# Six plain up tiles kept in SBUF, and the adaLN halves of the w_o stage spread over earlier stages

## The chip, the cores and the metric

One core of one Trainium2 chip. The metric is the device time of one execution in microseconds; the kernel before was run three times, and its median counts. Beside the times stands a profile of one execution, with every instruction's engine, source line, start and duration. Its engines are PE (TensorE, matrix products), PEld (its weight loads), DVE (VectorE), ACT (ScalarE), POOL (GpSimd, here an issuer of DMAs) and SP (SyncE, which issues most DMAs). An engine works its instructions off in the order in which they were compiled; an instruction that waits holds all behind it on its engine.

## What is computed

One layer of a decoder trunk for 512 tokens and 2048 channels, in float32: a mixing sub-layer (two attention groups) and a gated MLP with a short causal convolution, each with adaLN modulation from a vector `c`.

```python
mod = silu(c) @ w_ada + b_ada                   # six rows of 2048: sh1, sc1, gt1, sh2, sc2, gt2
h = rmsnorm(x, g_mix) * (1 + sc1) + sh1
x = x + (1 + gt1) * mixer(h, ...)               # ends in: merged @ w_o
h = rmsnorm(x, g_ffn) * (1 + sc2) + sh2
u = h @ w_up                                    # 2048 x 11264
u = conv_b + conv_w[0]*u[t-2] + conv_w[1]*u[t-1] + conv_w[2]*u[t]
a, b = split(u)
x = x + (1 + gt2) * ((silu(a) * b) @ w_down)
out = rmsnorm(x, g_final)
```

The last row of `mod` (gt2) is made in another place (`last_gate`) and is not touched.

## The kernel before

**Products.** Activations lie channels by tokens (128 x 512 tiles). Each float32 product is made of three passes on high and low parts (`mm3`, lines 176 to 180). A weight piece of 128 x 1024 comes by a DMA from SP into one of eight `raw` buffers; ACT copies its high part into `wh` (L168), and DVE subtracts to get `wl` (L170); there are three rooms of `wh` and `wl`, used in turn.

**A unit** (`unit`, lines 242 to 315) makes two output tiles `c1` and `c2` from two columns of weights and the 16 operand tiles, by seven half-size products of 24 matmuls with 256 columns each (a Strassen-like scheme). It loads four weight quarters `a11`, `a21`, `a22`, `a12` and keeps a fifth `raw` buffer `s` for sums of them (L268, L272; L306 and L310 work in place). It evacuates with ACT (L266, L270, L304) and DVE (L276, L308, L309, L312, L314). Twice, after its second product and after its fourth, it calls `between(i, *pins)`, where other stages hang side work; `behind(*pins)` places that work in its engine's order behind the named instructions. PSUM has three banks `acc`, four `att` and one `outs`; units use `acc` and `att` in turn.

**Order.** The program is traced in the order of the code, and a scheduler at compile time fixes each engine's order, by priority of tracing and by when operands and free buffers are expected. A tile gets a buffer of its tag when one is free: `raw` has eight, `F` (from `slot()`) 62 of 128 x 512, `T` two. The operand forms of a unit stage hold 56 of the 62 slots.

**adaLN halves.** `mod` is computed by DVE: a row tile of `w_ada` (128 x 1024, half of one of 48 tiles) is loaded into a `raw` buffer (`ada_load`, L702) and multiplied and summed against `cb[half]` (`some_ada`, L711). There are 96 halves from `ada_left`, first halves first. `cb[1]`, the second half of silu(c) on all partitions, takes one `raw` buffer from the first second half to the last. Before the change, 31 of them are done in the w_x units (one per unit), 7 through the `soft` buffer beside them, 15 in the stick-breaking heads 0 to 4, 26 in the sparse heads, 6 in the w_b stage and the last 11 in the w_o units (`between`, lines 1119 to 1123, up to two per unit).

**Stages, in order:** values and index queries (to about 232 us), 31 w_x units (to about 826), indexer and values (`indexer`, lines 873 to 880), eight stick-breaking heads (to about 1003), eight sparse heads with `branch_a` beside them (to about 1138), w_b, eight w_o units (first evacuation at 1235), the first up stage, 41 up units (first evacuations from 1478 to 2266), the down stages.

**First up stage** (lines 1223 to 1295). Six up tiles (three `a`, three `b` tiles, 2 x `NU`) are made by plain products in six PSUM banks (`ups`). ACT evacuates them to slots (L405), and POOL saves them to DRAM (`ud`, L1295). Later `finish_first` brings each back by SP's queue (L1337), applies the convolution (L1330 on ACT, L1333 twice on DVE), Silu (L1346), the product of the pair (L1352), and saves the result to `yd`. One step of it is traced per up unit from j = 9 on, 27 steps in all.

**Up units** (lines 1357 to 1364). For each pair the unit's outputs go through `finish` (convolution L1210 on ACT, L1211 and L1212 on DVE, Silu L1217, product L1219). `beside_up` hangs a step of `last_gate` and `turn` into each call; `turn` transposes an x1 tile (four transposes into `outs`) and frees its slot. Tiles 14 and 15 are read back from DRAM into `T` buffers for that at j = 6 and 7; tile 13 is still in a slot when the w_o stage ends and is turned in the first up unit.

Of the kernel before, what the change touches and what calls it, by code (L numbers as in the profile page):

```python
# [14 lines left out]
AF = mybir.ActivationFunctionType  # L15
ALU = mybir.AluOpType
# [4 lines left out]
S = 512  # L21
KT = D // P
# [14 lines left out]
NU = 3  # L37
# [39 lines left out]
def block_kernel(ctx: ExitStack, tc: tile.TileContext, A: dict, out: bass.AP):  # L77
    nc = tc.nc
# [10 lines left out]
    def t2k(tag, bufs, dt=F32, w=S):  # L89
        return sb.tile([P, w], dt, tag=tag, bufs=bufs, name=nm(tag))  # L90

    def slot(dt=F32):

        return t2k("F", SLOTS, dt)
# [11 lines left out]
    act = nc.scalar.activation  # L106
    tt = nc.vector.tensor_tensor
    ts = nc.vector.tensor_scalar
    stt = nc.vector.scalar_tensor_tensor
# [213 lines left out]
    @contextmanager  # L323
    def behind(*pins):

        with ExitStack() as stack:
            for p in pins:
                stack.enter_context(tc.issue_after(p.ins))
            yield
# [73 lines left out]
    def evac(ps, rows=slice(0, P), scale=None):  # L403
        o = slot()
        act(o[rows], ps[rows], AF.Copy, **({} if scale is None else {"scale": scale}))  # L405
        return o
# [6 lines left out]
    for k in range(KT):  # L413
# [4 lines left out]
        t = KT + k  # L418
# [4 lines left out]
        x = xt[k]  # L423
# [34 lines left out]
    dram = lambda name, n, w=S: [dr.tile([P, w], F32, tag=f"{name}{i}", name=f"{name}{i}") for i in range(n)]  # L458
    save = nc.gpsimd.dma_start
# [18 lines left out]
    for k in range(KT):  # L478
# [4 lines left out]
        if k == 0:  # L483
# [3 lines left out]
            w = w_next  # L487
        else:
            with behind(*([ada_tile(k + 1)] if k + 1 < KT else [])):
                tt(lo, xt[k], hi.bitcast(F32), ALU.subtract)  # L490
            w = prep(A["w_qi"][k])
# [20 lines left out]
    ps = acc()  # L512
    for c in range(2):
        w = prep(A["w_tail"][c], 8 * TN)
# [12 lines left out]
    for j, (src, dst) in enumerate(((A["w_x0"][0], xd[0]), (A["w_x0"][1], xd[1]))):  # L527
        ps = (acc, att)[j % 2]()
        for c in range(2):
            w = prep(src[c])  # L530
            for k in range(8):
                i = 8 * c + k
# [162 lines left out]
    def ada_load(n=1, tag=("raw", 8)):  # L695
        for _ in range(min(n, len(ada_left))):
            t, half = ada_left.pop(0)
            if half and cb[1] is None:
                cb[1] = t2k("raw", 8, w=1024)
                nc.sync.dma_start(cb[1], c_half.to_broadcast([P, 1024]))  # L700
            w = t2k(*tag, w=1024)
            nc.sync.dma_start(w, A["w_ada"][t * P : (t + 1) * P, half * 1024 : (half + 1) * 1024])  # L702
            ada_ready.append((w, t, half))

    def some_ada(n=1):
        for _ in range(n):
            if not ada_ready:
                ada_load()
            if ada_ready:
                w, t, half = ada_ready.pop(0)  # L710
                stt(w, w, 1.0, cb[half], ALU.mult, ALU.mult, accum_out=macc[:, t, half : half + 1])  # L711
# [36 lines left out]
    for u in range(1, 32):  # L748

        def between(i, *pins):  # L750
            if not i:
                ada_load()
            with behind(*pins):
                next(work)
                if i:
                    some_ada()

        pair = unit(A["w_x"][u - 1], f, between)
        for i, o in enumerate(pair):
            if u >= 16:  # L760
                sig = act(o, o, AF.Sigmoid)
            save(xd[2 * u + i], o)
# [42 lines left out]
    bias = [causal]  # L805
# [61 lines left out]
    def run(work, n=1):  # L867
        for _ in range(n):
            last = next(work, None)
        return last  # L870
# [4 lines left out]
    run(index)  # L875
    fill = values(0, vb[0])
    for i in range(16):
        run(fill, 2)
        run(index)
    run(fill)  # L880


# [136 lines left out]
    def sparse_3(p):  # L1019
        tps = [acc() for _ in range(3)]  # L1020
        tp = strips(*tps)
        pT = t2k("w", 2), t2k("T", 2), t2k("T", 2)
        for b in (2, 0, 1, 3):
            for kb in range(b + 1):
                nc.tensor.transpose(tp[b][:, kb * P : (kb + 1) * P], p[b][:, kb * P : (kb + 1) * P], ident)
        for n in (1, 2, 0):
            W = (S, S, 2 * P)[n]
            act(pT[n][:, :W], tps[n][:, :W], AF.Copy)
        return strips(*pT)
# [27 lines left out]
    for hd in range(NH):  # L1057
        ada_load(2 if hd > 1 else 0)
        p, s, last = sparse_1(*pairs[hd])
        if before:  # L1060
            sparse_4(*before, y)
        if hd + 1 < NH:
            pairs.append(turned(hd + 1))
        run(fill)
        with behind(last):
            some_ada(2 if hd > 1 else 0)
        ada_load(2 if hd else 0)
        last = sparse_2(p, s)
        run(fill)
        before = hd, sparse_3(p), vb[hd // 4]  # L1070
        with behind(last):
            some_ada(2 if hd else 0)
        run(fill, 2)
    sparse_4(*before, y)
    run(fill)
# [7 lines left out]
    for j in range(KT):  # L1083
        t = t2k("w", 2)
# [3 lines left out]
        ps = acc()  # L1088
        w = prep(A["w_b"][j])
# [16 lines left out]
    to_turn = []  # L1106

    def turn():

        if to_turn:  # L1110
            j, x = to_turn.pop(0)
            ps = outs()
            for b in range(NQB):
                nc.tensor.transpose(ps[:, b * P : (b + 1) * P], x[:, b * P : (b + 1) * P], ident)
            o = slot()
            act(o, ps, AF.Copy)
            save(x1t[:, :, j * P : (j + 1) * P], o.rearrange("p (b f) -> p b f", b=NQB))

    def between(i, *pins):
        turn()  # L1120
        with behind(*pins):
            some_ada()
        ada_load()

    def residual(c, j, x, at=slice(0, S)):
        stt(c[:, at], c[:, at], mod[:, 32 + j : 33 + j], x[:, at], ALU.mult, ALU.add)
# [163 lines left out]
    for form in (form_t, form_u):  # L1290
        for p in range(KT // 2 - LAG, KT // 2):
            form(f[p], x1[2 * p], x1[2 * p + 1])
    ud = dram("ud", 2 * NU)
    for i, ps in enumerate(ups):
        save(ud[i], evac(ps))  # L1295

    gate_row = dr.tile([1, D], F32, tag="gate", name="gate")
    gate_sum = [dr.tile([P, 1024], F32, tag=f"gates{half}", name=f"gates{half}") for half in range(2)]
# [1 line left out]
    def last_gate():  # L1300
# [9 lines left out]
        for b in range(4):  # L1310
# [7 lines left out]
            save(gate_row[:, b * S : (b + 1) * S], w[:1, S:])  # L1318
            yield

    def beside_up(i, *pins):
        turn()
        with behind(*pins):
            run(gate)

    def finish_first():

        def half(j, u):
            t = t2k("T", 2)
            act(t, u, AF.Identity, scale=cw[:, j, 2:3], bias=cw[:, j, 3:4])  # L1330
            for i in (1, 2):
                yield t
                stt(t[:, i:], u[:, : S - i], cw[:, j, 2 - i : 3 - i], t[:, i:], ALU.mult, ALU.add)  # L1333

        def bring(i):
            u = slot()
            nc.sync.dma_start(u, ud[i])  # L1337
            return u

        for j in range(NU):  # L1340
            u = bring(2 * j)
            yield
            yield
            for a in half(2 * j, u):
                yield
            act(a, a, AF.Silu)  # L1346
            u = bring(2 * j + 1)
            yield
            yield
            for b in half(2 * j + 1, u):  # L1350
                yield
            tt(a, a, b, ALU.mult)  # L1352
            save(yd[j // 2][:, j % 2 * S : (j % 2 + 1) * S], a)
            yield

    gate, first_tiles = last_gate(), finish_first()
    for j in range(NU, NJ):
        if 2 * NU <= j < 2 * NU + 2:
            x = t2k("T", 2)
            save(x, x1d[KT - 2 + j - 2 * NU])  # L1360
            to_turn.append((KT - 2 + j - 2 * NU, x))
        if j >= 3 * NU:
            run(first_tiles)
        finish(j, *unit(A["w_up"][j - NU], f, beside_up))


# [365 lines left out]
```

## Time and profile before

| what | value |
|---|---|
| median of three runs | 2738.51 us (2733.37 to 2740.41) |
| the profiled execution | 2737.63 us |
| its span, first to last instruction | 2735.7 us |
| granted TensorE clock, mean | 0.995 |
| TensorE matmuls | 18700 |
| issues of `w_ada` rows into `raw` | 152 of 512 KB |
| issues to and from `ud` | 6 and 6 of 256 KB |

How to read the rows below: a windows row gives a stretch of the span, its length, each engine's busy time with the number of instructions, the granted clock, the DMA engines' share and their rate. A row of the lines or the waits view names the line, engine and tiles; `X <- Y: 5.2, 2, 2.9` says that X waited for Y 5.2 us in total, two times, 2.9 us at most. A timeline row gives start, duration, engine, line, operation, and in brackets the engine's idle time before it and what ended that.

### The profile page before, as it was taken

How to read it: one execution, taken by the hardware profiler on the slowest of the kernel's cores; microseconds unless marked ns; L12 is line 12 of the kernel's file. 1: busy time of each engine (PE TensorE's matmuls, PEld its weight loads, DVE VectorE, ACT ScalarE, POOL GpSimd, SP SyncE). 2: the span in 40 equal slices, each digit the busy share in tenths (PEclk: the TensorE clock that was granted, in tenths of full speed). 3: DMA queues.
4: the chain of work that ended last, by engine and by line, in shares of the span. 5: the costliest groups of instructions: out<-in, count | busy, mean ns of one | idle time of the engine just before them, and what ended most of it. 6: DMA issues, size and time to landing. Idle time of an engine off the chain costs nothing.

```text
span 2735.7 us, 47661 instructions
## 1 busy us (share of the span) xinstructions
PE 2677.8 (98%) x18700; PEld 2453.8 (90%) x18700; DVE 2406.6 (88%) x3402; ACT 1448.4 (53%) x2037; POOL 315.8 (12%) x514
## 2 busy tenths in 40 slices
PE   8999999999999999999999999999999999999998
PEld 6789999999997778889999999999999998887876
DVE  8888989999987899798878999999999997888887
ACT  4444455554446665434466555555555455546443
POOL 0000010100012211112220000000000000003011
PEclk9999999999999999999999999999999999999999
DMA  9883556666676648766864666666666436468785
GB/s 351 326 301 123 174 199 196 192 212 220 205 227 203 199 140 285 237 206 216 243 215 136 189 175 189 173 181 175 171 177 181 132 125 223 154 179 236 207 228 166
DMA packets 167853, 551.65 MB, mean 202 GB/s; under 512 B 21750, under 2 KB 22390, under 8 KB 167628
## 3 DMA queue, kind: packets, MB, share of 16 engines
q1 hardware_dynamic: 119820, 408.49, 46.4%
q0 software_dynamic: 47216, 139.73, 18.7%
q8 instruction: 147, 2.41, 0.3%
q14 instruction: 78, 0.64, 0.1%
q10 hardware_dynamic: 592, 0.39, 0.1%
HBM read 453.97 MB, written 91.14 MB: 199 GB/s over the span
## 4 chain that ended last, share of the span: by engine, by line
PE 83%; DVE 8%; DMA 4%; issue 3%; ACT 2%; SPq 0%; POOL 0%; ACTq 0%; DVEq 0%; POOLq 0%
PE att L180 13%; PE att L179 13%; PE att L178 13%; PE acc L179 12%; PE acc L180 12%; PE acc L178 12%; DVE wl L170 2%; PE acc L928 1%; DMA F<-ud 1%; ACT wh L168 1%; DMA raw<-in_w_down 1%; PE outs L179 1%; PE outs L178 1%; PE outs L180 1%; PE acc L896 1%
## 5 line engine op out<-in xcount | busy, mean ns | idle before, releaser
L168 ACT ACTIVATE wh<-raw 128x1024 fp32r<-128x1024 f32 (+1 forms) x790 | 828.8, 1055 | 945.7 <-DVE raw L272 174.9
L170 DVE TENSOR_TENSOR wl<-raw,wh 128x1024 fp32r<-128x1024 f32 (+1 forms) x790 | 953.4, 1214 | 125.3 <-ACT wh L168 117.7
L178 PE MATMUL acc<-F,wh 128*128 128x256 f32 (+1 forms) x2448 | 702.3, 287 | 9.0 <-DVE sp L308 4.3
L178 PE MATMUL att<-F,wh 128*128 128x256 f32 (+1 forms) x2448 | 704.3, 288 | 6.2 <-DVE sp L308 5.2
L180 PE MATMUL acc<-F,wl 128*128 128x256 f32 (+1 forms) x2448 | 701.5, 287 | 8.1 <-DVE wl L170 8.1
L180 PE MATMUL att<-F,wl 128*128 128x256 f32 (+1 forms) x2448 | 702.3, 287 | 4.3 <-DVE wl L170 4.3
L179 PE MATMUL att<-F,wh 128*128 128x256 f32 (+1 forms) x2448 | 701.6, 287 | 0.2 <-DVE F L199 0.2
L179 PE MATMUL acc<-F,wh 128*128 128x256 f32 (+1 forms) x2448 | 701.2, 287 | 0.1
L178 PEld LDWEIGHTS acc<-F,wh 128*128 128x128 f32 x2448 | 460.2, 188 | 21.8 <-issue 5.1
L178 PEld LDWEIGHTS att<-F,wh 128*128 128x128 f32 x2448 | 461.6, 189 | 17.4 <-issue 5.7
L180 PEld LDWEIGHTS acc<-F,wl 128*128 128x128 f32 x2448 | 460.4, 188 | 18.1 <-DVE wl L170 9.3
L180 PEld LDWEIGHTS att<-F,wl 128*128 128x128 f32 x2448 | 461.7, 189 | 13.2 <-DVE wl L170 5.0
L179 PEld LDWEIGHTS att<-F,wh 128*128 128x128 f32 x2448 | 461.7, 189 | 8.8 <-DVE F L199 0.7
L179 PEld LDWEIGHTS acc<-F,wh 128*128 128x128 f32 x2448 | 460.5, 188 | 10.1 <-DVE F L490 0.8
L178 PE MATMUL att<-wh,F 128*128 128x512 f32 x448 | 177.8, 398 | 0.2 <-ACT wh L168 0.2
L179 PE MATMUL att<-wl,F 128*128 128x512 f32 x448 | 175.3, 391 | 0.7 <-DVE wl L170 0.7
L180 PE MATMUL att<-wh,F 128*128 128x512 f32 x448 | 175.1, 391 | 0.0
L179 PE MATMUL acc<-wl,F 128*128 128x512 f32 x288 | 113.5, 394 | 4.3 <-DVE wl L170 4.3
L268 DVE TENSOR_TENSOR raw<-raw,raw 128x1024 f32<-128x1024 f32 x80 | 97.4, 1218 | 18.9 <-DMA raw<-in_w_o 14.1
L178 PE MATMUL acc<-wh,F 128*128 128x512 f32 x288 | 112.4, 393 | 0.1
L180 PE MATMUL acc<-wh,F 128*128 128x512 f32 x288 | 111.3, 391 | 0.0
L711 DVE SCALAR_TENSOR_TENSOR raw<-raw,raw 128x1024 f32<-128x1024 f32 x89 | 107.3, 1217 | 0.8 <-DMA raw<-in_w_ada 0.8
(370 smaller groups left out, 3719.9 us busy)
## 6 DMA issues: line engine op xcount, KB each, us to landing
raw<-in_w_up SPq DMA_DIRECT2D x164, 512.0 KB, 3.8
raw<-in_w_ada SPq DMA_DIRECT2D x152, 512.0 KB, 5.2
raw<-in_w_x SPq DMA_DIRECT2D x128, 512.0 KB, 4.3
raw<-in_w_down SPq DMA_DIRECT2D x104, 512.0 KB, 4.5
xd<-F POOLq DMA_DIRECT2D x64, 256.0 KB, 3.0
F<-xd POOLq DMA_DIRECT2D x64, 256.0 KB, 4.9
raw<-in_w_o SPq DMA_DIRECT2D x32, 512.0 KB, 5.5
soft<-in_w_gate SPq DMA_DIRECT2D x32, 512.0 KB, 3.9
```

Source lines behind the costliest of these rows:

```text
L168: pins["wh"] = act(wh, raw, AF.Copy)
L170: pins["wl"] = tt(wl, raw, wh.bitcast(F32), ALU.subtract)
L178: mm(ps, ah, bh, start=first, stop=False, skip_group_check=not check)
L179: mm(ps, ah, bl, start=False, stop=False, skip_group_check=not check)
L180: return mm(ps, al, bh, start=False, stop=last, skip_group_check=not check)
L268: last_v = tt(s, a21, a22, ALU.add)
L711: stt(w, w, 1.0, cb[half], ALU.mult, ALU.mult, accum_out=macc[:, t, half : half + 1])
L896: mm(zk, k[:, q0 : q0 + P], q[:, q0:], start=kb != 3, stop=False, skip_group_check=True)
L928: mm(o, negtri if tri else negones, i, start=False, stop=True, skip_group_check=True)
```

## The change

Four of the six plain up tiles stay in slots and two in one `raw` buffer (`wide`), and nothing of them goes to DRAM. `finish_steps` does the same arithmetic in 15 steps (four convolution steps and one product for each of three pairs), one at each call of `beside_up`, so two per unit from the first up unit on. `turn` is not called in the first nine up units; tiles 14 and 15 are read back at j = 12 and 13.

The adaLN halves: w_x units 29 and 30 load five and do five (three more than before), the loop around the indexer two, sparse heads 6 and 7 three more each. `between` of w_o now asks for one half per unit instead of two; by then `ada_left` is empty.

```diff
@@ w_x units
         def between(i, *pins):
+            free = u in (29, 30)
             if not i:
+                ada_load(2 if free else 1)
+            elif u == 29:
                 ada_load()
             with behind(*pins):
                 next(work)
-                if i:
-                    some_ada()
+                if i or u == 30:
+                    some_ada(2 if free and i else 1)
@@ indexer and values
     for i in range(16):
+        if i in (3, 9):
+            ada_load()
         run(fill, 2)
         run(index)
+        if i in (6, 12):
+            some_ada()
@@ sparse heads
         run(fill)
+        if hd > 5:
+            ada_load(3)
         before = hd, sparse_3(p), vb[hd // 4]
         with behind(last):
-            some_ada(2 if hd else 0)
+            some_ada((2 if hd else 0) + (3 if hd > 5 else 0))
@@ w_o units
     def between(i, *pins):
         turn()
         with behind(*pins):
-            some_ada()
-        ada_load()
+            if i:
+                some_ada()
+        if not i:
+            ada_load()
@@ first up stage
-    ud = dram("ud", 2 * NU)
-    for i, ps in enumerate(ups):
-        save(ud[i], evac(ps))
+    wide = t2k("raw", 8, w=1024)
+    banks, ups = ups, [evac(ps) for ps in ups[:4]]
+    for i in range(2):
+        ups.append(wide[:, i * S : (i + 1) * S])
+        act(ups[-1], banks[4 + i], AF.Copy)
@@ up units
+    def finish_steps():
+
+        for j in range(NU):
+            out = [t2k("T", 2) for _ in range(2)]
+            for a, t in enumerate(out):
+                u, c = ups[2 * j + a], 2 * j + a
+                act(t, u, AF.Identity, scale=cw[:, c, 2:3], bias=cw[:, c, 3:4])
+                for i in (1, 2):
+                    stt(t[:, i:], u[:, : S - i], cw[:, c, 2 - i : 3 - i], t[:, i:], ALU.mult, ALU.add)
+                    if i == 2 and a == 0:
+                        act(t, t, AF.Silu)
+                    yield
+            a, b = out
+            tt(a, a, b, ALU.mult)
+            nc.gpsimd.dma_start(yd[j // 2][:, j % 2 * S : (j % 2 + 1) * S], a)
+            yield
+
     def beside_up(i, *pins):
-        turn()
+        if j >= 4 * NU:
+            turn()
         with behind(*pins):
+            run(first_tiles)
             run(gate)
...
-    gate, first_tiles = last_gate(), finish_first()
+    gate, first_tiles = last_gate(), finish_steps()
     for j in range(NU, NJ):
-        if 2 * NU <= j < 2 * NU + 2:
+        if 4 * NU <= j < 4 * NU + 2:
             x = t2k("T", 2)
-            save(x, x1d[KT - 2 + j - 2 * NU])
-            to_turn.append((KT - 2 + j - 2 * NU, x))
-        if j >= 3 * NU:
-            run(first_tiles)
+            save(x, x1d[KT - 2 + j - 4 * NU])
+            to_turn.append((KT - 2 + j - 4 * NU, x))
         finish(j, *unit(A["w_up"][j - NU], f, beside_up))
```

`finish_first` is removed with its loads.

More of the change, by code (lines that the diff above doesn't have):

```diff
@@ L1319, in last_gate @@
             yield
+    def finish_steps():
[13 more added lines that the diff above has]
+            yield
     def beside_up(i, *pins):
-        turn()
+        if j >= 4 * NU:
+            turn()
         with behind(*pins):
+            run(first_tiles)
             run(gate)
[L1326 to L1354, printed above, removed]
-    gate, first_tiles = last_gate(), finish_first()
+    gate, first_tiles = last_gate(), finish_steps()
     for j in range(NU, NJ):
-        if 2 * NU <= j < 2 * NU + 2:
+        if 4 * NU <= j < 4 * NU + 2:
             x = t2k("T", 2)
-            save(x, x1d[KT - 2 + j - 2 * NU])
-            to_turn.append((KT - 2 + j - 2 * NU, x))
-        if j >= 3 * NU:
-            run(first_tiles)
+            save(x, x1d[KT - 2 + j - 4 * NU])
+            to_turn.append((KT - 2 + j - 4 * NU, x))
         finish(j, *unit(A["w_up"][j - NU], f, beside_up))
```

## Prediction, before the change was run

> **What bounds the kernel now.** I read the page first (busy times), then TensorE's pace unit by unit with the windows view, then the waits view of the two stages that the change touches, and last the timeline of one stall in each.
>
> ```profile
> span 2735.7 us, 47661 instructions
> PE 2677.8 (98%) x18700; PEld 2453.8 (90%) x18700; DVE 2406.6 (88%) x3402; ACT 1448.4 (53%) x2037; POOL 315.8 (12%) x514
> ```
>
> TensorE is the bound. Nothing here makes a matmul cheaper or removes one, so a change can gain only where TensorE stops. DVE at 88% is close behind: a stop is nearly always DVE or ACT being late. The next windows each run from the first evacuation (L266) of one up unit to that of a later one; the first holds one undisturbed unit, the six others two units each.
>
> ```profile
> core 0: us, PE busy (x) PEld busy (x) DVE busy (x) ACT busy (x) POOL busy (x), PEclk, DMA share, GB/s
> 1711.20:1730.24 19.04, 19.04 (x171) 19.04 (x170) 17.84 (x22) 10.99 (x16) 1.43 (x2) 1.00 0.67 178
> 1574.88:1614.88 40.00, 38.44 (x339) 38.24 (x338) 36.83 (x45) 23.30 (x31) 2.83 (x4) 1.00 0.63 176
> 1652.90:1692.21 39.31, 38.73 (x342) 38.53 (x341) 37.25 (x46) 22.68 (x30) 3.39 (x5) 1.00 0.67 188
> 1749.28:1791.92 42.64, 40.26 (x339) 39.87 (x338) 37.09 (x45) 23.18 (x31) 2.83 (x4) 0.96 0.62 168
> 1829.95:1873.06 43.11, 40.30 (x339) 39.90 (x338) 37.53 (x46) 22.68 (x30) 3.39 (x5) 0.96 0.62 172
> 1930.18:1972.11 41.93, 40.08 (x339) 39.89 (x338) 37.10 (x45) 23.20 (x32) 2.84 (x4) 0.96 0.63 170
> 2010.13:2051.46 41.33, 39.00 (x342) 38.60 (x341) 37.25 (x46) 22.67 (x31) 3.40 (x5) 1.00 0.65 179
> ```
>
> An undisturbed unit takes 19.04 us: 168 matmuls, 113 ns apart. Two take 38.08, so the six windows are 1.92, 1.23, 4.56, 5.03, 3.85 and 3.25 us too long, **19.8 us** together. Six stalls, and the old finishing loads exactly six tiles back from DRAM. The waits view and the timeline of the third join them:
>
> ```profile
> ACT T L1330 <- DMA F<-ud: 25.8, 6, 5.3
> PE acc L180 <- DVE wl L170: 6.1, 4, 2.1
> PE att L180 <- DVE wl L170: 4.3, 2, 2.1
> ```
>
> ```profile
> 1768.58 0.82 ACT L1330 ACTIVATE T<-F,cw 128x512 f32<-128x512 f32 x1 [4.90 <-DMA F<-ud]
> 1773.03 0.58 PE L180 MATMUL att<-F,wl 128*128 128x256 f32 x1 [2.13 <-DVE wl L170]
> 1773.40 0.41 PE L178 MATMUL att<-F,wh 128*128 128x256 f32 x1
> ...
> 1775.96 0.41 PE L178 MATMUL att<-F,wh 128*128 128x256 f32 x1
> ```
>
> The reader of the load stands in ACT's queue too early: ACT sits still for 4.90 us, with the next weight splits (`wh`, L168) behind it. DVE needs `wh` for `wl`, so TensorE stops 2.13 us. Afterwards 12 matmuls take 1773.40 to 1775.96, 213 ns apart instead of 113: a stop is also paid in clock. The windows hold both parts of that loss.
>
> The second place is the w_o stage (1205 to 1345), PE's and DVE's waits:
>
> ```profile
> PE att L178 <- DVE sp L308: 5.2, 2, 2.9
> PE acc L178 <- DVE F L1092: 2.4, 1, 2.4
> PE acc L180 <- DVE wl L170: 1.3, 1, 1.3
> PE acc L178 <- DVE sp L308: 1.1, 1, 1.1
> DVE raw L268 <- DMA raw<-in_w_o: 14.1, 5, 4.6
> DVE raw L711 <- DMA raw<-in_w_ada: 0.8, 1, 0.8
> ```
>
> ```profile
> 1310.14 1.23 DVE L268 TENSOR_TENSOR raw<-raw,raw 128x1024 f32<-128x1024 f32 x1 [4.64 <-DMA raw<-in_w_o]
> ```
>
> ```profile
> 1298.79:1322.93 24.14, 21.29 (x173) 21.12 (x172) 19.18 (x24) 10.38 (x16) 6.29 (x10) 0.93 0.77 234
> ```
>
> A unit uses five of the eight `raw` buffers (four loads and `s`). Here `cb[1]` holds one and adaLN rows one or two, so w_o quarters are issued late, DVE waits for them (14.1 us, five times), and then still has an adaLN half (L711) in front of what TensorE needs (L308). TensorE's waits are 10.0 us (5.2 + 2.4 + 1.3 + 1.1); the unit with clock 0.93 adds about 1.5 us.
>
> **The change, part by part.**
>
> *Plain up tiles.* Gone: six saves of 256 KB on POOL's queue, six loads on SP's, and ACT's 25.8 us of waits for them. The six evacuations stay (two go to a `raw` buffer). Gain 19.8 us. What is late next there: nothing; the 19.04 us units around the stalls show no PE stop.
>
> The finishing work stays, but now comes two steps per unit in eight units instead of about one in 27.
>
> ```profile
> L1333 DVE SCALAR_TENSOR_TENSOR T<-F,cw,T x12: 741/744/750, 1604.7 to 2042.8; 128x511 f32<-128x511 f32 x6, 128x510 f32<-128x510 f32 x6
> L1352 DVE TENSOR_TENSOR T<-T,T x3: 679/683/684, 1684.5 to 2043.8; 128x512 f32<-128x512 f32 x3
> 1478.23:1499.17 20.94, 20.94 (x187) 20.94 (x186) 16.92 (x19) 12.03 (x16) 1.27 (x2) 1.00 0.54 176
> 638.49:657.52 19.03, 19.03 (x171) 19.03 (x170) 18.39 (x23) 9.17 (x13) 1.08 (x2) 1.00 0.67 222
> ```
>
> On DVE 12 x 0.744 + 3 x 0.683 = 11.0 us, on ACT 6 x 0.82 (the row at 1768.58) plus three Silu, under 7.5 us, beside eight units. ACT is busy 11 of 19 us, so it has room. DVE has 19.04 - 17.84 = 1.20 us per unit, and 20.94 - 16.92 = 4.0 us in the first one, which has no convolution of its own yet: 4.0 + 7 x 1.2 = 12.4 us of room for 11.0 us of work. It fits in sum, but not in each unit: after the first, 9.5 us of steps meet 8.4 us of room. The unit at 638.49 shows that DVE busy for 18.39 us still gives full pace; beyond that no row shows it. Lower end: 0, because `wl` is made up to two products ahead (three rooms) and takes up the difference. Upper end: if the 0.65 us that DVE idles even there (19.03 - 18.39) can't be used, 7 x 0.65 + 1.1 = 5.7 us are missing, and one stop more in clock as above (1.2 us, 12 x 0.1) makes 7. I take **2.0 us**, near the lower end, because the row nearest to it lost nothing.
>
> The Trainium skill (TensorE: Matmul & The Clock Gate, "Why this matters for your kernels") advises against idle gaps of more than about 3 us, since a longer one halves the clock; by it a stop of 2 us would cost only itself, and the upper end would be 5.7 instead of 7. The trace does not agree: 213 ns follow a stop of 2.13 us.
>
> The steps' waits: step 1's DVE operation waits for its own ACT operation, and queued behind it stands a `wl`; ACT's copy is 0.8 us and ACT has just been free. Slots: 56 for the operands, 4 plain tiles, one for x1 tile 13 (turned only at j = 12 now) leave one of 62 for two outputs; the second comes free when the first plain tile is done, which is in the same unit and on the same engine (DVE) that writes the output. Cost 0 as long as convolutions aren't late; the rival below prices it. That `raw` has seven buffers in these units costs 0: the w_x units keep an adaLN row in one and run at 19.03 us.
>
> *w_o without adaLN.* From the code: of 96 halves, w_x took 31 and `soft` 7, the sticks 15, the sparse heads 26, w_b 6, so w_o had 11. Now w_x has 34, the indexer 2, sparse 32, and **w_o none**; `cb[1]` is free before it. All eight `raw` buffers serve w_o, as they serve w_up, where L268 never waits for weights:
>
> ```profile
> L268 DVE TENSOR_TENSOR raw<-raw,raw 128x1024 f32<-128x1024 f32 x80 | 97.4, 1218 | 18.9 <-DMA raw<-in_w_o 14.1 <-DMA rope<-raw 4.4 <-DMA raw<-in_w_x 0.3
> ```
>
> Of the 11.5 us of loss the L308 stops (5.2 + 1.1 + 1.5 of clock) go whole. Before 1231, DVE loses a half and its wait (1.22 + 0.81), so of 2.4 us 0.4 stay; of the `wl` stop of 1.3 us about 0.2 stay behind a half of 1.22. That is 10.9 us; I take **10**, since w_o has its DMA share at 0.77 and may wait once. Ends: 5 (the two stops of the transition stay, 3.7, and the longest of L308, 2.9) and 11.5.
>
> *Where the 11 halves go.* Each is a 512 KB load on SP and 1.22 + 0.08 us on DVE.
>
> ```profile
> 772.46:792.38 19.92, 19.92 (x172) 19.44 (x171) 16.21 (x18) 9.77 (x15) 5.27 (x7) 1.00 0.81 205
> 792.38:811.61 19.23, 19.23 (x172) 19.23 (x171) 18.06 (x22) 9.29 (x14) 1.08 (x2) 1.00 0.75 250
> 811.61:830.65 19.04, 19.04 (x153) 18.36 (x152) 16.00 (x22) 9.49 (x14) 2.17 (x4) 1.00 0.82 271
> 840.00:860.00 20.00, 20.00 (x91) 15.38 (x90) 12.67 (x21) 11.97 (x21) 6.15 (x12) 1.00 0.70 248
> ...
> 1119.08 0.69 DVE L1049 TENSOR_TENSOR F<-att,F 128x512 f32<-128x512 f32 x1 [4.43 <-PE att L180]
> 1135.52 0.69 DVE L1049 TENSOR_TENSOR F<-att,F 128x512 f32<-128x512 f32 x1 [4.43 <-PE att L180]
> ```
>
> Unit 29 takes one more (3.7 us of room), unit 30 two (2.6 us into 1.2), and unit 31 with 3.0 us of room clears the rest. For these two units SP's queue holds up to three adaLN loads ahead of weights: 0 if the buffers suffice, 4 us if each loses what a w_o unit loses (about 2 us: 7.8 of L308 in four units); I take **1**. The indexer takes 2.6 us where DVE idles 7.3 of 20 us: 0, at most 2.6. Sparse heads 6 and 7 take three each, 3.9 us into the idle 4.43 us: 0, at most 3 if a load lands late; it would hold DVE with the next head's maxima behind it.
>
> **Sum.** 2735.7 - 19.8 + 2.0 - 10 + 1.0 = 2708.9 us of span. The profiled execution took 2737.63, 1.93 more than its span, and the median is 2738.51, 0.88 above it: **2712 us**, 1.0% less.
>
> **Rivals.**
>
> A. *Buffers run short in the up units.* `wide` holds one `raw` until step 15. If w_up needs all eight, each of 7.5 units loses the 2 us of a w_o unit: 15 us, so 2727. Against it: w_x above. The Trainium skill (Perfetto Trace Analysis, "Identifying Performance Opportunities") speaks for it: gaps that repeat on the busiest engine can mean too few buffers, and the five waits for w_o bear it out. A DVE shortage at its upper end (7) lands between.
>
> B. *The moved halves stall where they land*: 4 + 2.6 + 3, about 10 us: 2721.
>
> C. *Slower: convolutions hold the output slots.* With one slot too few, L304 (ACT) of a unit needs the slot that the previous unit's convolution (L1212, DVE) reads.
>
> ```profile
> 1750.84 0.74 DVE L1212 SCALAR_TENSOR_TENSOR w<-F,cw,w 128x510 f32<-128x510 f32 x1
> 1757.61 0.36 ACT L304 ACTIVATE F<-acc 128x256 f32<-128x256 f32 x1
> ```
>
> The margin is 1757.61 - 1751.58 = 6.0 us. Should the steps push convolutions back by more than that, ACT stands still with `wh` behind it, as for the DRAM loads, and each of eight units loses up to 4.6 us (the third window): 36 us, 2748.
>
> D. *The change doesn't do what it says*: the stops of ACT were only the place where some other lateness showed, and as much comes back: 2731 to 2747. Against it: 19.04 us units on both sides of every load.
>
> **How the numbers follow.** The forecast (2704 to 2720) 0.62, A 0.14, B 0.12, D 0.06, C 0.06. The lowest time is 2735.7 - 19.8 - 11.5 + 2.8, about 2707, and I leave 4 us below it for matmuls that come earlier in other stages; the top takes in A and B: 2703 to 2729. A measurement tells about 0.3% (8 us) from no change; faster by more than that is below 2730: the forecast, B, and most of A, 0.85; within it 0.08; slower 0.07.
>
> **What would show it.** Right: no `F<-ud`; up units of 19.04 us from the fourth on, except where tiles are turned or the gate row is summed; no wait of L268 for w_o and no L711 after 1215; w_o units of about 19 to 20 us. Wrong: L268 waiting for `in_w_up` in the first eight up units (A), `wl` waits there (DVE short), ACT waiting before L304 (C), new stops at 780 to 830 or 1100 to 1140 (B).

## The result, and the profile after

The kernel after takes **2720.71 us** (median of four, 2717.62 to 2722.9) against 2739.19 us for the kernel before (2733.37 to 2740.41): ratio 0.9936, 95% interval 0.9917 to 0.9955. That is 18.5 us faster. The forecast was 2712 us, 26.5 less than the 2738.51 it started from; so the sign and the range held, and about a third of the gain is missing. A second measurement beside another set of runs (e11 below) gave 2718.42 us against 2736.45: 18.0 us, ratio 0.9939 (0.9927 to 0.9952).

The page's first line, after:

```profile
span 2721.1 us, 47620 instructions
```

The windows below cut the middle of the span at first evacuations (L266) of units. Of before they are: indexer to sparse heads and w_b (units 31 to 32), the w_o units (32 to 38), the last w_o unit with the plain tiles and up units 40 and 41, units 42 to 44, 45 to 48, 49 to 71.

```profile
811.61:1235.31 423.70, 418.23 (x2051) 332.61 (x2049) 367.32 (x733) 230.56 (x397) 73.42 (x137) 1.00 0.64 213
1235.31:1381.86 146.55, 138.91 (x1196) 137.90 (x1195) 124.26 (x151) 71.01 (x97) 33.93 (x50) 0.99 0.74 224
1381.86:1516.79 134.93, 132.72 (x1000) 126.81 (x999) 111.59 (x189) 86.55 (x138) 19.07 (x34) 0.99 0.54 178
1516.79:1574.88 58.09, 58.09 (x515) 58.09 (x514) 53.56 (x64) 34.18 (x46) 5.75 (x8) 1.00 0.70 186
1574.88:1652.90 78.02, 76.46 (x675) 76.26 (x674) 72.44 (x87) 45.28 (x59) 5.67 (x8) 1.00 0.64 178
1652.90:2108.52 455.62, 445.69 (x3867) 443.73 (x3866) 417.91 (x497) 257.25 (x331) 34.37 (x49) 0.99 0.65 178
```

The same stretches after, with units 29 and 30 in front (19.92 + 19.23 = 39.15 us before):

```profile
769.96:814.05 44.09, 41.53 (x346) 40.89 (x345) 36.93 (x46) 19.30 (x27) 6.36 (x9) 0.96 0.82 242
814.05:1238.34 424.29, 418.48 (x2046) 332.24 (x2045) 375.83 (x750) 230.38 (x397) 73.57 (x137) 1.00 0.66 222
1238.34:1374.70 136.36, 136.20 (x1196) 135.86 (x1195) 114.24 (x128) 71.11 (x98) 33.91 (x50) 1.00 0.68 197
1374.70:1519.14 144.44, 138.35 (x1006) 130.99 (x1004) 113.48 (x194) 88.10 (x140) 14.62 (x26) 0.96 0.45 151
1519.14:1576.39 57.25, 57.04 (x501) 56.69 (x500) 56.35 (x69) 35.04 (x46) 4.83 (x7) 1.00 0.63 175
1576.39:1655.59 79.20, 77.47 (x675) 76.62 (x674) 74.22 (x90) 46.60 (x62) 8.08 (x12) 1.00 0.68 193
1655.59:2094.45 438.86, 438.86 (x3875) 438.86 (x3874) 410.30 (x484) 253.84 (x326) 34.14 (x48) 1.00 0.66 181
```

| stretch | after minus before, us |
|---|---|
| units 29 and 30 | +4.9 |
| indexer, sticks, sparse heads, w_b | +0.6 |
| w_o units 32 to 38 | -10.2 |
| last w_o unit, plain tiles, units 40 and 41 | +9.5 |
| units 42 to 44 | -0.8 |
| units 45 to 48 | +1.2 |
| units 49 to 71 | -16.8 |

Together -11.6 us. A further 2.5 us, which the two traces differ by already at unit 29 (772.46 against 769.96), lie in w_x units that the change doesn't touch, and are chance (e11, the same program as after, has 772.07), and 0.5 us of the 14.6 between the two spans lie behind unit 71. The two gains of the forecast are there in full: no `F<-ud` is left, PE is busy for the whole of units 49 to 71, and w_o runs without the waits for its weights. The waits of PE in w_o (1205 to 1345), and the group of L268, after:

```profile
PE acc L178 <- DVE F L1101: 1.0, 1, 1.0
```

```profile
L268 DVE TENSOR_TENSOR raw<-raw,raw 128x1024 f32<-128x1024 f32 x80 | 97.2, 1215 | 8.2 <-DMA raw<-in_w_x 4.0 <-DMA rope<-raw 3.9
```

The 14.1 us of waits for `in_w_o` are gone, but L268 now waits 4.0 us for `in_w_x`, where it had waited 0.3. So the missing part was paid in places that the forecast had put at 1, 0 and 2 us: unit 29, the start of the up units, and units 45 to 48.

### The profile page after: what moved, and what is told of

It reads as the page before. It is cut to its first block, busy times and chain, and to the rows that moved or that the text cites. A ratio compares the mean times of both kernels' runs of the same rounds, so it can differ in the third digit from the quotient of the medians.

```text
span 2721.1 us, 47620 instructions
## 1 busy us (share of the span) xinstructions
PE 2675.3 (98%) x18700; PEld 2450.3 (90%) x18700; DVE 2406.3 (88%) x3402; ACT 1448.5 (53%) x2037; POOL 313.1 (12%) x508
## 4 chain that ended last, share of the span: by engine, by line
PE 79%; DVE 7%; issue 7%; DMA 3%; ACT 2%; POOL 1%; SPq 0%; ACTq 0%; DVEq 0%; POOLq 0%
PE att L178 12%; PE att L180 12%; PE att L179 12%; PE acc L180 12%; PE acc L178 12%; PE acc L179 12%; DVE wl L170 2%; DMA raw<-in_w_down 1%; PE outs L1042 1%; PE outs L179 1%; PE outs L178 1%; PE outs L180 1%; PE acc L1011 1%; ACT wh L168 1%; DVE F L199 1%
## 5 line engine op out<-in xcount | busy, mean ns | idle before, releaser
L268 DVE TENSOR_TENSOR raw<-raw,raw 128x1024 f32<-128x1024 f32 x80 | 97.2, 1215 | 8.2 <-DMA raw<-in_w_x 4.0
```

Source lines behind the costliest of these rows:

```text
L268: last_v = tt(s, a21, a22, ALU.add)
```

## The experiments

All times are medians with those of the kernel before on the same chip beside them. In the expectations, "theory T" is the first reading of the two traces: each term's size is the shift of the same instruction from one trace to the other.

### e1 and e2: the two halves of the change alone

e1 is the kernel before with the adaLN part of the diff and nothing else. e2 is the kernel after without it:

```diff
 e1, against before: the hunks of the w_x units, the indexer,
 the sparse heads and w_o's between
 e2, against before: wide, finish_steps, beside_up and the loop of the up units
```

> The kernel before with the adaLN moves alone: units 29 and 30, the indexer and sparse heads 6 and 7 take the halves of w_o; the six plain tiles still go out to ud and come back. By the prediction: w_o -10, units 29 and 30 +1, indexer and heads 0, so 9 us under the kernel before. By the instruction shifts between the two traces (theory T): w_o -11.7, units 29 to 31 +4.9, indexer +2.1, so 4.7 us under it. If the moves and the plain tiles influence each other (rival), the shift at the start of the sparse heads is not +7, or w_o does not come out near 18 to 20 us a unit.

> The kernel after without the adaLN moves: the plain tiles stay on chip, w_o and the places before it are as in the kernel before. By the prediction: -19.8 for the ud stalls and +2 for the denser steps, 17.8 us under the kernel before. By theory T: -16.5 for the stalls that go, +8 at the start of the up units, 8 to 10 us under it. With e1 it should add up to the gain of the whole change, 15 to 18 us; if it doesn't, the two halves of the change touch each other. The stops of the start (1.3 us ahead of the first wh of unit 40, then the waits of units 40 and 41) should stand in its trace as in that of after, since nothing ahead of them in w_o causes them.

e1: 2728.94 us against 2736.45, ratio 0.9976 (0.9963 to 0.9988). e2: 2727.33 us, ratio 0.9971 (0.9960 to 0.9982). The two gains, 7.5 and 9.1 us, add up to 16.6, within the uncertainty of the 18.0 to 18.5 of the whole: no effect of one half on the other is to be seen. The interval of e1's gain (3.3 to 10.1 us) holds both the prediction's 9 and theory T's 4.7; e2's 9.1 us is what theory T said, and about half of the prediction's 17.8. Windows of e1 (units 29 and 30; w_o; the start; units 49 to 71):

```profile
770.25:814.20 43.95, 41.46 (x346) 40.81 (x345) 36.94 (x46) 19.29 (x26) 6.37 (x9) 0.96 0.83 244
1237.51:1373.90 136.39, 136.23 (x1196) 135.89 (x1195) 114.26 (x128) 71.13 (x98) 33.92 (x50) 1.00 0.69 197
1373.90:1507.28 133.38, 131.17 (x1000) 125.27 (x999) 111.57 (x189) 86.50 (x137) 19.11 (x34) 1.00 0.56 181
1645.67:2097.08 451.41, 440.49 (x3867) 438.75 (x3866) 416.99 (x497) 257.54 (x331) 34.42 (x49) 1.00 0.65 179
```

and of e2 (the start; its units 49 to 71 take 438.86 us as in after):

```profile
1381.66:1521.86 140.20, 133.85 (x1006) 126.57 (x1004) 113.57 (x194) 88.17 (x140) 14.62 (x26) 1.00 0.47 155
```

The adaLN half has both the loss in units 29 and 30 (4.8 us here) and the 10.2 us of gain in w_o. The plain-tile half has the loss at the start: 140.2 us where before has 134.9 and e1 133.4, so 5.3 to 6.8 us. Theory T had taken 8 us for it from one trace; part of that was not the kernel's doing (e11). The stalls of the `ud` loads also vary: units 49 to 71 are 455.6 us in before and 451.4 in e1, with the same code there; so what is won there by removing them is 12.6 to 16.8 us. Part of that is only another share-out among the stalls: units 45 to 71, which hold all six, take 533.6 us in before (78.02 + 455.62) and 531.7 in e1 (80.29 + 451.41). In e6 below, where nothing stops in them, they take 515.0 (76.16 + 438.86), which makes 16.7 to 18.6 us.

### e3 and e10: units 29 and 30

e3 gives both units back what they had before; e10 only unit 29.

```diff
 e3, against after
-            free = u in (29, 30)
             if not i:
-                ada_load(2 if free else 1)
-            elif u == 29:
                 ada_load()
...
-        if hd > 5:
+        if hd > 4:
             ada_load(3)
 e10, against after
-            free = u in (29, 30)
+            free = u == 30
...
-            elif u == 29:
-                ada_load()
...
-                if i or u == 30:
-                    some_ada(2 if free and i else 1)
+                if i:
+                    some_ada(2 if free else 1)
...
+        more = (0, 0, 0, 0, 0, 2, 3, 3)[hd]
```

> The kernel after, but units 29 and 30 take only what they took in the kernel before; the three halves more go to sparse head 5. By theory T the 4.9 us that units 29 to 31 lost come back and head 5 costs nothing, as heads 6 and 7 did: 4 to 5 us under after. By the prediction, which gave these units 1 us: at most 1 us under after. If head 5 has no room (rival), its span grows by up to 3 us and less than 2 us are won.

> The kernel after, but unit 29 takes only what it took in the kernel before; unit 30 still takes one half more (two loads at its first place), and two halves go to sparse head 5. If the 4.5 us of unit 29 come from its own third adaLN load, which leaves its weight quarters late: unit 29 is back at 19.92 us and unit 30 loses at most 0.7 us, 4 to 5 us under after. If they come from any unit there that has two adaLN loads ahead of weights (rival): unit 30 now loses 2 to 4 us and little is won.

e3: 2715.75 us against 2736.45, ratio 0.9933 (0.9920 to 0.9945). e10: 2717.65 against 2736.45, ratio 0.9934 (0.9916 to 0.9951), beside 2718.42 for the kernel after. The times alone can't tell either from after; the traces can. In e3 units 29 and 30 take 19.92 and 19.04 us. Windows of the same two units in e10:

```profile
771.64:791.56 19.92, 19.92 (x172) 19.44 (x171) 16.21 (x18) 9.77 (x14) 5.27 (x7) 1.00 0.79 206
791.56:811.25 19.69, 19.69 (x176) 19.69 (x175) 18.80 (x24) 9.41 (x14) 1.08 (x2) 1.00 0.83 280
```

Of the 4.9 us, 4.5 are unit 29's own, from two loads and one half more than before, and they go with these; unit 30, with two loads at once, loses half a microsecond. The timeline of SP shows why. In the kernel after, three adaLN loads stand ahead of unit 30's quarters:

```profile
758.19 10.77 SPq L702 DMA_DIRECT2D raw<-in_w_ada  x3
772.64 5.80 SPq L154 DMA_DIRECT2D raw<-in_w_x  x4
```

SP's own waits (757 to 773) have `SPq L702 <- DVE raw L306: 7.7, 1, 7.7`: one of these loads stood 7.7 us in the queue until DVE had done L306 and with it a `raw` buffer came free; the quarters stood behind it. In e10, whose unit 29 begins 1.68 us later, the first quarter is issued 10.5 us earlier:

```profile
762.14 13.92 SPq L154 DMA_DIRECT2D raw<-in_w_x  x4
```

With all four quarters issued only from 772.64 us on, behind the loads, the sum `s` of the next unit waits on DVE, and L308 of unit 29, which TensorE needs, stands behind it (timeline of DVE, after):

```profile
784.35 1.23 DVE L268 TENSOR_TENSOR raw<-raw,raw 128x1024 f32<-128x1024 f32 x1 [3.99 <-DMA raw<-in_w_x]
785.49 0.42 DVE L308 TENSOR_TENSOR sp<-att,ta 128x256 f32<-128x256 f32 x1
```

PE stops 2.6 us there, and the row of units 29 and 30 has a clock of 0.96: it is the pattern of the old w_o units, moved.

### e5: one raw buffer taken for two plain tiles, with no finishing step near

The kernel before, with the last two plain tiles in a `raw` buffer whose store to `ud` is traced only in unit 44:

```diff
-    for i, ps in enumerate(ups):
+    wide = t2k("raw", 8, w=1024)
+    for i, ps in enumerate(ups[:4]):
         save(ud[i], evac(ps))
+    for i in range(2):
+        act(wide[:, i * S : (i + 1) * S], ups[4 + i], AF.Copy)
...
+        if j == 2 * NU + 1:
+            save(ud[4 + i], wide[:, i * S : (i + 1) * S])
```

> The kernel before with one thing added: the last two plain tiles are copied to a raw buffer that is held until unit 44, and are stored to ud from there; the finishing steps stay where they were, behind three rounds of units. The theory that the missing raw buffer alone makes the slow start (theory R): the stops at the start of unit 40 appear here too, 4 to 6 us over the kernel before between the last w_o unit and unit 44, although no finishing step runs there. Rival S (the finishing steps, one at each side place, crowd VectorE and ScalarE): the start is as in the kernel before, within 1 us.

2739.65 us against 2736.72, ratio 1.0011 (0.9999 to 1.0024): by its time alone e5 can't be told from before. The stretch from unit 39 to 42 takes 138.6 us, 3.7 more than in before (at a clock of 0.99) and 5.2 more than in e1 (at 1.00, as in e5), and PE waits (1455 to 1530), where before and e1 have no wait at all:

```profile
1385.24:1523.84 138.60, 133.23 (x1004) 126.11 (x1003) 111.15 (x189) 86.68 (x138) 19.10 (x34) 1.00 0.54 173
PE acc L178 <- ACT wh L168: 1.7, 3, 1.2
PE acc L180 <- DVE wl L170: 0.8, 1, 0.8
PE outs L1114 <- ACT F L1116: 0.7, 1, 0.7
```

ScalarE's timeline says how. First the kernel before, around the six evacuations (L405):

```profile
1465.99 1.06 ACT L168 ACTIVATE wh<-raw 128x1024 fp32r<-128x1024 f32 x1 [1.01 <-PE att L1233]
...
1470.47 1.06 ACT L168 ACTIVATE wh<-raw 128x1024 fp32r<-128x1024 f32 x1 [2.90 <-PE att L1233]
1471.43 1.76 ACT L405 ACTIVATE F<-acc 128x512 f32<-128x512 f32 x3
```

Then e11 (the kernel after once more), and e5:

```profile
1463.32 1.97 ACT L405 ACTIVATE F<-acc 128x512 f32<-128x512 f32 x3 [5.65 <-PE acc L1245]
...
1466.05 1.28 ACT L1308 ACTIVATE raw<-att 128x512 f32<-128x512 f32 x2
1467.23 1.05 ACT L168 ACTIVATE wh<-raw 128x1024 fp32r<-128x1024 f32 x1
```

```profile
1473.05 1.97 ACT L405 ACTIVATE F<-acc 128x512 f32<-128x512 f32 x3 [5.65 <-PE acc L1234]
...
1475.79 1.28 ACT L1298 ACTIVATE raw<-att 128x512 f32<-128x512 f32 x2
...
1477.44 1.06 ACT L168 ACTIVATE wh<-raw 128x1024 fp32r<-128x1024 f32 x1
```

The 1024-wide `wh` are those of the up units (the plain stage's are 768 wide). Before has two of them ahead of the evacuations, and they are made while the plain products still run. With one `raw` taken, ACT sits still for 5.65 us, then evacuates, and only then makes the first `wh` of unit 40. The idle time, the evacuations and the copies of e5 and of e11 agree to the hundredth (5.65, 1.97 and 1.28), though e5 has no finishing step there.

The buffer was not held to unit 44, though. The compiled order put both stores right behind the copies, the second at 1478.49 (timeline of POOL, the first):

```profile
1476.68 0.54 POOL L1329 DMA_DIRECT2D ud<-raw  x1
```

SP's next load, which waited for it (`SPq L154 <- DMA ud<-raw: 15.4, 1, 15.4`), had the buffer at 1481.58, ahead of unit 40's first evacuation at 1482.64. So `wide` and its two copies, taken across the end of the plain stage alone, are enough to make the late start of unit 40; neither the steps nor a long hold is needed for it. The buffer was not tried without the copies. Nor were the weights late: the first four 1024-wide loads, as many as unit 40 needs, were issued by 1453.0 in e5 and by 1443.2 in e11, 24 us ahead of the first `wh` in each, and the waits of 1440 to 1660 have none for `in_w_up` in either. The weights lie there, and the evacuations stand ahead of them in ScalarE's order.

### e4: unit 40's first parts traced ahead of the evacuations

```diff
+    ahead = load(A["w_up"][0][0])
+    ahead = ahead, parts(ahead, 1024, True)
...
-        finish(j, *unit(A["w_up"][j - NU], f, beside_up))
+        finish(j, *unit(A["w_up"][j - NU], f, beside_up, ahead=ahead if j == NU else None))
```

> The kernel after with the first quarter of unit 40 loaded and its hi and lo parts made ahead of the six evacuations in program order, so that ScalarE and VectorE meet these parts before the evacuations. Theory T (the long-lived wide buffer takes a raw early, each load of unit 40 comes one release later, and in ScalarE's order the evacuations stand ahead of unit 40's first wh): the stop of 1.35 us at the first wh and some of the waits after it go, 3 to 8 us under after. Rival (one step per side place makes VectorE and ScalarE late in units 40 and 41): at most 1.5 us under after. Second rival (the loads themselves are late, since wide holds a raw): the parts still wait for the quarter and the stop stays, 0 to 1.5 us under after.

2717.5 us against 2736.45, ratio 0.9936 (0.9923 to 0.9949): no different from after. PE's waits for the acc banks (1455 to 1530) in e11, and the two of unit 41 behind them:

```profile
PE acc L178 <- ACT wh L168: 2.4, 2, 1.2
PE acc L180 <- DVE wl L170: 1.0, 2, 0.8
PE att L178 <- ACT wh L168: 0.6, 1, 0.6
PE att L178 <- DVE sp L308: 0.3, 1, 0.3
```

and in e4:

```profile
PE acc L178 <- ACT wh L168: 1.4, 2, 1.0
...
PE acc L180 <- DVE wl L170: 0.2, 1, 0.2
```

The waits fell by 1.8 us, from 4.3 to 2.5, so ScalarE's order is part of the mechanism; but only the first of unit 40's parts was put right, and the rest still came late (units 39 to 41 take 139.8 us, at a clock of 0.99, against 140.1 in e11 at 1.00). The theory's 3 to 8 us fall.

### e7: the two tiles left in their PSUM banks

No `wide`, no copies: the last pair is finished first, straight from PSUM, two steps at each side place of unit 40.

```diff
-    wide = t2k("raw", 8, w=1024)
-    banks, ups = ups, [evac(ps) for ps in ups[:4]]
-    for i in range(2):
-        ups.append(wide[:, i * S : (i + 1) * S])
-        act(ups[-1], banks[4 + i], AF.Copy)
+    ups = [evac(ps) for ps in ups[:4]] + ups[4:]
...
-        for j in range(NU):
+        for j in (2, 0, 1):
...
-            run(first_tiles)
+            run(first_tiles, 2 if j == NU else 1)
```

> The kernel after without the wide buffer: the last two plain tiles are not copied at all, they stay in their two PSUM banks and are finished from there first, two steps at each side place of unit 40. No raw is held, two ScalarE copies go. Theory R: the stops at the start of unit 40 go, 4 to 5 us under after. Rival S: four steps in unit 40 instead of two, so the stops stay or grow: 0 to 3 us over after. Third case: unit 41's products wait for the banks, up to 2 us back.

2714.39 us against 2736.72, ratio 0.9921 (0.9903 to 0.9939). PE's waits from 1455 to 1530 are down from 4.3 us to one line:

```profile
PE acc L180 <- DVE wl L170: 0.6, 2, 0.4
```

ScalarE's order is that of before again: two 1024-wide `wh` (1461.78 and 1466.26) ahead of the evacuations (1467.22). The waits of the start are gone, with twice as many steps in unit 40: the rival that the steps crowd out the start falls. By its time alone e7 can't be told from after. The stop that after has in units 45 and 46 comes one unit earlier, in 44 and 45, and is no smaller.

### e6: fewer steps per unit

The kernel after with two steps a unit in units 40 to 42 and one in each unit behind them; the turns move back with them.

```diff
-            run(first_tiles)
+            if i or j < NU + 2:
+                run(first_tiles)
...
-        if 4 * NU <= j < 4 * NU + 2:
+        if 6 * NU <= j < 6 * NU + 2:
```

> The kernel after with two steps a unit in units 40 to 42 only and one step a unit behind them (the turns move back with them). Rival S: the later stops (0.9 us at unit 45 and what follows to unit 47) go, about 1.3 us under after, and the start stays. Theory R: the raw is held longer (steps end later), so units 43 to 51 lose up to 0.5 us each; the start stays: 0 to 4 us over after.

(By the code these are units 40 and 41, as `j` begins at `NU` = 3.) 2716.94 us against 2736.72, ratio 0.9929 (0.9912 to 0.9945). The row of units 45 and 46 of after, then of e6 units 45 to 48 and 45 and 46:

```profile
1576.39:1617.58 41.19, 39.46 (x339) 38.61 (x338) 38.61 (x48) 24.14 (x33) 3.94 (x6) 1.00 0.63 180
```

```profile
1570.79:1646.95 76.16, 76.16 (x675) 76.16 (x674) 73.32 (x89) 45.16 (x60) 6.25 (x9) 1.00 0.66 184
1570.79:1608.87 38.08, 38.08 (x339) 38.08 (x338) 36.69 (x45) 22.58 (x30) 2.84 (x4) 1.00 0.67 180
```

Four units at full pace: 76.16 instead of 79.20, so the denser steps cost **3.0 us** there. With DVE busy for 18.3 us a unit (36.69 / 2) nothing is lost. With 38.61 us of work for the 38.08 us of two units DVE can't keep up: PE's longest wait in after's units 45 and 46 is for L308 (0.8 us). It doesn't begin there: after's units 42 to 44 have DVE busy for 56.35 of 57.25 us with hardly a stop. The room made by parts prepared ahead is used up first and paid for in units 45 and 46. That the raw is held longer in e6 (last read at 1691.6 us, in e11 at 1600.4) costs nothing: behind the start there is room for it.

### e8 and e9: a version that beats both

e8 is e7 and e3, and the indexer's two halves go to sparse head 4. e9 adds the thinner steps, and the turns move back as in e6.

```diff
 e8, against e7 and e3
-        if i in (3, 9):
-            ada_load()
-        if i in (6, 12):
-            some_ada()
...
+        more = (0, 0, 0, 0, 2, 3, 3, 3)[hd]
...
 e9, against e8
-            run(first_tiles, 2 if j == NU else 1)
+            if i or j < NU + 3:
+                run(first_tiles, 2 if j == NU else 1)
...
```

> e7 and e3 together, and the indexer gives its two halves up too: sparse heads 4 to 7 take 2, 3, 3 and 3 halves more, units 29 and 30 and the indexer are as in the kernel before. By the instruction shifts: 4.9 us (units 29 to 31) and 1.2 to 2.1 us (indexer) under after, and 4 to 5 us for the start if theory R holds: 10 to 12 us under after. Without theory R 6 to 7 us under after. If head 4 has no room, 2 us less.

> e8 with the thinner steps of e6: four steps in unit 40, two in units 41 and 42, one in each unit behind them; turns moved back. If what e6 won (3.0 us in units 45 to 48) and what e8 won add up: 3 us under e8, about 11 us under the kernel after, with no stop over 0.3 us in units 43 to 70. If the two plain tiles of the later pairs, which now wait longer in their slots, hold the operands' slots (rival), units 43 to 48 stay longer than 19.04 us: 0 to 2 us under e8.

e8: 2708.95 us against 2736.72, ratio 0.9901 (0.9883 to 0.9920). e9: **2707.86 us** against 2736.45, ratio 0.9896 (0.9881 to 0.9912): 10.6 us under the kernel after in the same set (2718.42, ratio 0.9939 from 0.9927), and the intervals don't meet. Windows of e8 (indexer to w_b; the start) and e9 (units 43 to 48):

```profile
809.37:1232.90 423.53, 418.65 (x2051) 332.76 (x2050) 378.55 (x756) 230.49 (x397) 73.39 (x137) 1.00 0.67 227
1369.34:1503.68 134.34, 131.73 (x1001) 125.59 (x1000) 115.48 (x196) 87.54 (x139) 14.60 (x26) 1.00 0.50 166
```

```profile
1529.01:1643.25 114.24, 114.24 (x1011) 114.24 (x1010) 109.99 (x133) 67.62 (x89) 9.06 (x13) 1.00 0.67 183
```

The start, with the clock at 1.00 as in e2, is 134.3 us instead of 140.2; in e7 and e9 it is 137.4, at 0.98. In e9, six units stand at six times 19.04. The indexer's halves were not worth moving: 423.5 us without them, 422.95 in e11 with them, and e9, without them again, has 425.4. The 2.1 us that the first reading of the traces had put there are within this scatter. By the times e8 and e9 can't be told apart; unit by unit, e9 has 3.0 us less in units 42 to 48.

### e11: the kernel after once more

> The kernel after once more, unchanged, beside e9 and e10 on the same chip: 16 to 20 us under the kernel before. Its stretch from the last w_o unit to unit 40 took 101.29 us in the first trace and 95 to 98 us in all the other kernels; if that was a matter of the clock in that one execution, it is 95 to 98 us here, and the span is 3 to 5 us shorter.

2718.42 us against 2736.45, span 2716.5. The start was 140.1 us (1375.51 to 1515.64) where the first trace had 144.4. Two windows of 18 us, from 18 us behind the last w_o unit's first evacuation, in the first trace and in e11:

```profile
1392.70:1410.70 18.00, 16.20 (x101) 15.57 (x102) 9.63 (x26) 8.55 (x19) 2.18 (x4) 0.81 0.67 242
```

```profile
1393.51:1411.51 18.00, 16.19 (x126) 15.56 (x127) 12.71 (x32) 11.32 (x23) 2.22 (x5) 1.00 0.70 260
```

The same program, the same stops, and a fifth fewer matmuls in the same time: the 4.3 us between the two are clock, not the change.

## Why the prediction was right, and where it was not

- **The `ud` stalls, -19.8 us: right.** 16.8 us in units 49 to 71, and 1.9 in units 45 to 48 (78.02 in before, 76.16 in e6). "What is late next there: nothing" holds: after's units 49 to 71 have no stop. With the same code there, before and e1 differ by 1.9 us over units 45 to 71, which a sum from one trace can't show.
- **w_o, -10 us: right.** 10.2 us in the seven units, with the waits for `in_w_o` gone and every middle unit at 20.0 us.
- **Indexer and sparse heads at 0: right.** 424.3 and 422.95 us with the halves, 423.7 before. Head 5 and head 4 had the same room (424.3 us in e3, 423.5 in e8).
- **"That `raw` has seven buffers in these units costs 0": wrong, at the start alone.** The argument came from w_x units in steady state, where one held buffer indeed does no harm, and e6 shows the same for the up units. The start is another case: there unit 40 is prepared while the plain products still run, and ScalarE's compiled order decides how far. e5 shows that `wide` makes the stop in unit 40 with no finishing step near (3.7 to 5.2 us), e7 that PE's waits there fall from 4.3 to 0.6 us without it. This is rival A's buffer, at one place instead of 7.5 units, but not rival A's path: its sign, L268 waiting for `in_w_up`, is in neither trace of the kernel after; the weights had landed and stood behind the evacuations. The advice behind that rival, the Trainium skill, Perfetto Trace Analysis, "Identifying Performance Opportunities", that repeated gaps can mean too few buffers, doesn't reach this case: here the gap came only once, between two stages.
- **Units 29 and 30 at 1 us: mis-sized, 4.9.** The step gave them "0 if the buffers suffice, 4 us if each loses what a w_o unit loses", and chose low. The buffers did not suffice (the wait of 7.7 us for one, under e3 and e10), and one unit alone lost 4.5. The mechanism had been shown in the forecast itself, in w_o; unit 29 has a DMA share of 0.81 already before, where w_o had 0.77, and the choice of a low value had no row behind it. This is half of rival B's price, at one of its three places.
- **Denser steps at 2.0 us: mis-sized, 3.0** in units 45 to 48. Whether the 0.6 and 0.3 us of e11's waits on att banks in unit 41 are theirs too is open: e5, without steps, has no stop there, but neither has e7, which has the steps and no held buffer. The ends of 0 and 7 hold the 3.0. The sum of 9.5 us of steps against 8.4 us of room was the better guide than the single unit at 18.39 us: one unit at that load lives on what was prepared ahead, and several in a row use it up.
- **Rival C did not come**: in the trace of after ACT has no idle time ahead of L304 at all, so no unit waited for a slot there.

In sum, the stretches with e11's start in place of the first trace's (140.13 - 134.93 = 5.2; against e1, at the same clock, 6.8) and without the indexer's row, which scatters: 4.9 - 10.2 + 5.2 - 0.8 + 1.2 - 16.8 = -16.5 us, near the 18.0 and 18.5 of the times. The forecast's -26.8 is larger by the 5.2 of the start, by 3.9 for unit 29 and 30 and by the 1.0 of the steps in units 45 to 48; these make -16.7.

What stays open: by which step `wide` changes ScalarE's order. The order is fixed when the kernel is compiled. The traces show that the weights weren't late; that the order makes the stop fits with e4, where tracing one load earlier took 1.8 us of waits away. Whether the buffer or the two copies into it move the evacuations ahead was not separated.

## What to carry to other kernels

A buffer that is taken across the seam between two stages is to be priced at the seam, not in a steady unit of the next stage: at the seam the next stage is prepared beside the end of the old one, and here the buffer with its two copies changed the order in which ScalarE did that (5.65 us of standing still, with the weights already there). Before work is put into "idle" places, look which loads it puts ahead of the weights there, and give it to a place whose engine waits on something else (the sparse heads took eleven halves for nothing, one more, with two loads more, cost 4.5 us in a w_x unit). Work that needs more than the room of an engine in each of several units in a row costs the difference, even if one unit at that load shows no loss; spread it.

## What was not expected of the hardware

The granted clock answered the same short stops differently from one execution to the next. PE's waits between 1375 and 1450, in e11:

```profile
PE acc L1244 <- DVE F L199: 1.0, 1, 1.0
PE outs L1165 <- DVE T L1162: 0.7, 1, 0.7
PE acc L1243 <- ACT F L197: 0.6, 1, 0.6
```

They are the same three, to the tenth, in the first trace of after. Yet the window quoted for e11 was at a clock of 0.81 in the one and of 1.00 in the other. The Trainium skill, TensorE: Matmul & The Clock Gate, "What's actually happening", describes the clock as set over a window that runs free of the kernel, so that the transition falls elsewhere each time; that agrees with the scatter. But that section ties the slow state to a whole idle window of about 3.4 us, and no stop here was half as long. Differences of 2 to 4 us between two traces of this kernel need a second trace before they are put down to code.
